# A decoder trunk on one core: a pinned prologue, the first scale on TensorE, and start-up units in sweeps

## The chip, the cores and the metric

The kernel runs on one core of a Trainium2 chip. The metric is the device time of one execution in microseconds, the median of several runs; smaller is better. The core's engines each run their own instructions in order and wait for each other by semaphores: TensorE (PE; its weight loads are shown as PEld), VectorE (DVE), ScalarE (ACT), GpSimd (POOL) and SyncE (SP), which issues all DMAs here.

## The reference

Two layers on x of 256 positions by 1024 channels. Each layer has three blocks: SwiGLU, a mixer (Mamba-2 in layer 0, block-sparse attention in layer 1), SwiGLU. Each block's input is normalized and modulated by a vector c:

```python
def modulate(x, g, c_act, w, b):
    m = c_act @ w + b
    shift, scale, gate = jnp.split(m, 3, axis=-1)
    h = rmsnorm(x, g) * (1.0 + scale[:, None, :]) + shift[:, None, :]
    return h, gate[:, None, :]

def swiglu(h, w_gate, w_up, w_down):
    return (jax.nn.silu(h @ w_gate) * (h @ w_up)) @ w_down
...
    c_act = jax.nn.silu(c)
    for i in range(DEPTH):
        h, g = modulate(x, norm_g[i, 0], c_act, mod_w[i, 0], mod_b[i, 0])
        x = x + 0.5 * g * swiglu(h, ffn_w_gate[i, 0], ffn_w_up[i, 0], ffn_w_down[i, 0])
...
    return rmsnorm(x, final_norm_g)
```

D_FF is 2816. All is float32.

## The kernel before

x lies transposed, channels on partitions: eight tiles of 128 channels by 256 positions. Every weight matrix is streamed once, in units of 16 blocks of 128 x 128 (1 MB), loaded by SP into three buffers `raw`. A product is kept near float32 accuracy by splitting both sides into a high part in a shorter format and the rest: `split` makes `hi` of a half unit (8 blocks, 128 x 1024) on ACT (line 309) and `lo = raw - hi` on DVE (line 316), and `make_x`, `pre_x` or, at the start, `first_x` make XH and XL of the activations. `prod` (lines 382 to 384) then issues three matmuls per block: hi by XH, hi by XL, lo by XH. Six `hi` and six `lo` buffers stand between the splits and TensorE.

The modulation vectors are made meanwhile: `modulation` multiplies a 128 x 1024 tile of the modulation matrix, `mraw`, by the broadcast c, `cb`, and sums along the row, in one instruction on DVE (line 340). `vectors` adds the bias (shift; line 325) or makes (acc + b1) * g (scale; line 327) into MV.

The first block cannot use vectors made ahead. So its first eight units (`ffn`, p == 0) go by input tile k: unit k holds the blocks of input tile k for eight output tiles m, gate and up. For each k a scale and a shift are made (tiles 8 + k and k), then `first_x` makes ut = x * scale * rb on DVE (line 1032), XH on ACT (line 1035) and XL on DVE (line 1036). `stream_order` sets the order of modulation tiles and units in ORDER; `pump` walks it, some half units ahead of TensorE; LOADS is the order of the DMAs.

Before that stands the prologue (the block "start"): the DMAs of V (vectors and biases), the identity and x; SiLU of c; eight transposes that broadcast c into two banks and two copies into `cb`; squares of x on ACT and DVE and their sums; eight one-column matmuls with `ones` (`rstd_sum`, line 393) for the mean square; the root on ACT (line 396) and four small DVE instructions; two transposes (`rstd_rows`) for the row vector `rb`. `early`, a manual schedule, is held from the start of this block to the first `pump`. From there on the scheduler sets the order of instructions on each engine by priority.

Of the kernel before, what the change touches and what calls it, by code (L numbers as in the profile page):

```python
# [146 lines left out]
def stream_order():  # L147
# [16 lines left out]
    for i in range(len(ALL_UNITS)):  # L164
        if i < NK:
            order += [("m", 0, 8 + i)] * (i < 2) + [("m", 0, i)] + [("m", 0, 9 + i)] * (1 <= i < NK - 1)
        order.append(("w", i))
        while n < len(items) and at[n] <= i + 1:
            order.append(("m",) + items[n])
            n += 1  # L170
# [7 lines left out]
LOADS += ORDER[3 * NK:3 * NK + 2] + [("c",)] + ORDER[3 * NK + 2:]  # L178
SLOT = {it: n % N_MOD for n, it in enumerate(it for it in LOADS if it[0] == "m")}
# [10 lines left out]

@with_exitstack
def hybrid_trunk(ctx, tc, w, mod, xt, vec, const, out, dbg=None):
# [3 lines left out]
    mm, act, dve, gps = nc.tensor, nc.scalar, nc.vector, nc.gpsimd  # L196
# [17 lines left out]
    b1 = pool.tile([128, 48], F32, name="b1")  # L214
    MV = pool.tile([128, 6, 3, NK], F32, name="MV")
# [10 lines left out]
    st = Core()  # L226
# [78 lines left out]
    def split(q):  # L305
# [45 lines left out]
    def pump(q):  # L351
# [3 lines left out]
        while st.s <= q:  # L355
# [29 lines left out]


    def rstd_sum(parts, n):
# [603 lines left out]
    with tc.tile_pool(name="start", bufs=1) as sp:  # L991
# [145 lines left out]
```

## Time and profile before

| what | us |
|---|---|
| median of 3 runs | 1114.82 |
| lowest and highest run | 1113.73, 1115.0 |
| the profiled execution | 1115.07 |
| its span | 1113.3 |
| PE busy | 1090.7 (98% of the span) |
| DVE busy | 897.4 (81%) |
| ACT busy | 602.4 (54%) |

The span goes from the first to the last instruction of the profiled execution; 1.77 us of its time lie around it. Ends of matmuls are modelled and overlap, so the spacing of their starts is what to read. In a timeline row the first number is the start, the second the duration; in brackets is the engine's idle time just before and what ended it. Instructions on DVE and ACT also overlap a little: the next can start before the last one's end. On the page, "us to landing" is from a DMA's issue to its data.

### The profile page before, as it was taken

To read this page: it belongs to the slowest core of one execution; us is meant where nothing else is said; L and a number is where in the kernel's file an instruction comes from. 1 tells how busy PE (TensorE), PEld (TensorE's weight loads), DVE (VectorE), ACT (ScalarE), POOL (GpSimd) and SP (SyncE) were. 2 spreads that over 40 slices of the span, in tenths; PEclk is the share of its full clock that TensorE was granted. 3 is DMA by queue.
4 is the path that set the end of the run, shared out by engine and by line. 5 is a ranking of instruction groups with operands and counts; after the bars stand their busy time and mean duration, and the time that the engine had idled before them with its cause. 6 is when DMAs were issued, how large, how long until landed. Compare 5 with 4: busy or idle time off the path is not lost.

```text
span 1113.3 us, 22076 instructions
## 1 busy us (share of the span) xinstructions
PE 1090.7 (98%) x9050; PEld 1067.7 (96%) x9050; DVE 897.4 (81%) x1445; ACT 602.4 (54%) x919; POOL 55.4 (5%) x61
## 2 busy tenths in 40 slices
PE   6999999999999998999999999999999999999997
PEld 6999999999899998999999999999988899999996
DVE  6998989899899999999976889886697779555542
ACT  4463445676776657444544644454475666444541
POOL 0000001000000001000001000001211210000010
PEclk9999999999999999999999999999999999999998
DMA  9989988853444663899966499986544336555531
GB/s 349 381 335 369 352 319 302 301 200 117 175 166 142 240 238 128 302 356 367 375 246 246 160 346 334 356 308 263 186 174 156 121 115 222 190 184 183 186 136 39
DMA packets 50358, 269.00 MB, mean 242 GB/s; under 512 B 5840, under 2 KB 6608, under 8 KB 28624
## 3 DMA queue, kind: packets, MB, share of 16 engines
q1 hardware_dynamic: 50256, 267.58, 65.4%
q8 instruction: 71, 1.16, 0.4%
q14 instruction: 31, 0.25, 0.1%
HBM read 266.51 MB, written 1.05 MB: 240 GB/s over the span
## 4 chain that ended last, share of the span: by engine, by line
PE 94%; DVE 4%; ACT 1%; issue 1%; DMA 0%; SPq 0%; DVEq 0%; ACTq 0%
PE bank L383 29%; PE bank L382 29%; PE bank L384 29%; PE bank L734 1%; DVE lo L316 1%; PE bank L957 1%; PE bank L959 1%; PE bank L958 1%; PE bank L874 1%; PE bank L393 1%; PE bank L915 1%; DVE x L458 0%; ACT hi L309 0%; DMA x<-in_xt_dram 0%; DVE X L439 0%
## 5 line engine op out<-in xcount | busy, mean ns | idle before, releaser
L316 DVE TENSOR_TENSOR lo<-raw,hi 128x1024 fp32r<-128x1024 f32 x361 | 437.7, 1221 | 136.9 <-ACT hi L309 136.6
L309 ACT ACTIVATE hi<-raw 128x1024 fp32r<-128x1024 f32 x361 | 376.8, 1057 | 310.8 <-PE bank L383 253.2
L383 PE MATMUL bank<-X,hi 128*128 128x256 f32 (+1 forms) x1928 | 542.7, 282 | 1.5 <-DVE X L439 1.4
L382 PE MATMUL bank<-X,hi 128*128 128x256 f32 (+1 forms) x1928 | 538.3, 282 | 4.0 <-ACT hi L309 2.5
L384 PE MATMUL bank<-X,lo 128*128 128x256 f32 (+1 forms) x1928 | 538.8, 281 | 0.2 <-DVE lo L316 0.2
L382 PEld LDWEIGHTS bank<-X,hi 128*128 128x128 f32 x1928 | 364.2, 190 | 8.6 <-issue 3.4
L383 PEld LDWEIGHTS bank<-X,hi 128*128 128x128 f32 x1928 | 363.7, 189 | 2.8 <-DVE X L439 1.8
L384 PEld LDWEIGHTS bank<-X,lo 128*128 128x128 f32 x1928 | 363.4, 189 | 0.4 <-DVE lo L316 0.4
L384 PE MATMUL bank<-H,lo 128*128 128x256 f32 x704 | 196.9, 280 | 0.0
L382 PE MATMUL bank<-H,hi 128*128 128x256 f32 x704 | 196.3, 279 | 0.0
L383 PE MATMUL bank<-H,hi 128*128 128x256 f32 x704 | 196.2, 279 | 0.0
L340 DVE SCALAR_TENSOR_TENSOR junk<-mraw,cb 128x1024 bf16<-128x1024 f32 x144 | 175.4, 1218 | 0.9 <-DMA mraw<-in_mod_dram 0.2
L383 PEld LDWEIGHTS bank<-H,hi 128*128 128x128 f32 x704 | 132.3, 188 | 0.0
L384 PEld LDWEIGHTS bank<-H,lo 128*128 128x128 f32 x704 | 132.1, 188 | 0.0
L382 PEld LDWEIGHTS bank<-H,hi 128*128 128x128 f32 x704 | 131.6, 187 | 0.0
L416 POOL TENSOR_TENSOR ssq<-ssq,sq 128x256 f32<-128x256 f32 x36 | 34.4, 955 | 966.3 <-ACT sq L414 965.8
L522 ACT ACTIVATE sg<-bank 128x512 f32<-128x512 f32 x41 | 24.0, 585 | 38.9 <-PE bank L384 38.9
L634 DVE SCALAR_TENSOR_TENSOR cv<-bank,V,cv 128x255 f32<-128x255 f32 (+2 forms) x96 | 44.3, 474 | 0.5
L458 DVE SCALAR_TENSOR_TENSOR x<-bank,MV,x 128x256 f32<-128x256 f32 x40 | 19.1, 480 | 29.2 <-PE bank L384 29.1
L414 ACT ACTIVATE sq<-x 128x256 f32<-128x256 f32 x36 | 14.9, 414 | 50.6 <-DVE x L458 45.9
L382 PE MATMUL bank<-GH,hi 128*128 128x256 f32 x128 | 36.2, 284 | 1.1 <-DVE cv L634 0.9
L384 PE MATMUL bank<-GH,lo 128*128 128x256 f32 x128 | 36.0, 282 | 0.0
(179 smaller groups left out, 924.1 us busy)
## 6 DMA issues: line engine op xcount, KB each, us to landing
raw<-in_w_dram SPq DMA_DIRECT2D x169, 1024.0 KB, 5.1
mraw<-in_mod_dram SPq DMA_DIRECT2D x144, 512.0 KB, 6.5
raw<-in_w_dram SPq DMA_DIRECT2D x23, 512.0 KB, 8.1
x<-in_xt_dram SPq DMA_DIRECT2D x2, 512.0 KB, 4.6
out_dram<-x SPq DMA_DIRECT2D x3, 256.0 KB, 2.3
out_dram<-x SPq DMA_DIRECT2D x2, 128.0 KB, 1.9
V<-in_vec_dram SPq DMA_DIRECT2D x1, 196.5 KB, 8.3
mask<-in_const_dram SPq DMA_DIRECT2D x1, 192.0 KB, 8.1
```

Of the source, the lines that this page charges most:

```text
L309: act.activation(h, r, AF.Copy)
L316: ins = dve.tensor_sub(l[:, c:wd], r[:, c:wd], h[:, c:wd].bitcast(F32)).ins
L340: ins = dve.scalar_tensor_tensor(junk, mraw[SLOT["m", j, c]], 1.0, cb, op0=OP.mult, op1=OP.mult, accum_out=acc[:, j, c:c + 1]).ins
L382: mm.matmul(ps, h, xh, start=start, stop=False, skip_group_check=True)
L383: mm.matmul(ps, h, xl, start=False, stop=False, skip_group_check=True)
L384: mm.matmul(ps, l, xh, start=False, stop=stop, skip_group_check=True)
L393: mm.matmul(ps[:, t:t + 1], s[:, 128 * t:128 * t + 128], ones[:, c:c + 1], start=e == 0 and t == 0, stop=e == len(parts) - 1, skip_group_c ...
L414: act.activation(s, src, AF.Square)
L416: gps.tensor_add(total, total, s)
L458: dve.scalar_tensor_tensor(x[:, d, :], ps, g, x[:, d, :], op0=OP.mult, op1=OP.add)
L522: act.activation(s, ps[:, :, :L], AF.Silu)
L634: dve.scalar_tensor_tensor(o[:, c, s:], ps[:, c, :L - s], V[:, wc + 3 - s:wc + 4 - s], o[:, c, s:], op0=OP.mult, op1=OP.add)
```

## The change

- The identity comes no longer by DMA: POOL fills it with ones and selects the diagonal (`affine_select`).
- The first scale (tile 8) is made by eight one-column matmuls on TensorE from its `mraw` tile and c; the host stores that tile transposed. It no longer needs DVE.
- Each half of the squares is summed to one 256-column tile by one more DVE addition, so the mean square takes four one-column matmuls and not eight. The load of the root's table moves ahead on ACT.
- 23 transposes into an unused bank (`warm`) are put between TensorE's steps of the prologue.
- The scale and shift of the eight input tiles are finished on ACT, (acc * g + b1 * g) and (acc + b), and not on DVE.
- In ORDER the scale product of unit k + 1 stands right behind the split of the first half of unit k, the shift product behind its second half.
- A wrapper, `Pinned`, keeps all instructions of PE, DVE and ACT in program order from the start until the second half of the last of the eight units. (All instructions that go through the wrapper show its line, L202, where the kernel's own line stood.)
- `sweeps` replaces `prod` in the eight units: for each half unit eight matmuls hi by XH, eight hi by XL, eight lo by XH.

```diff
@@ stream_order
         if i < NK:
-            order += [("m", 0, 8 + i)] * (i < 2) + [("m", 0, i)] + [("m", 0, 9 + i)] * (1 <= i < NK - 1)
-        order.append(("w", i))
+            order += [("m", 0, 8)] * (i == 0) + [("m", 0, i)]
+        order += [("w", i), ("m", 0, 9 + i)] if i < NK - 1 else [("w", i)]
@@
+class Pinned:
...
+        def call(*args, **kw):
+            ins = f(*args, **kw)
+            if self.st.pin:
+                self.tc.keep_in_program_order(ins)
+            return ins
+        return call
@@ hybrid_trunk
-    mm, act, dve, gps = nc.tensor, nc.scalar, nc.vector, nc.gpsimd
+    st = Core()
+    st.pin = False
+    mm, act, dve = (Pinned(tc, e, st) for e in (nc.tensor, nc.scalar, nc.vector))
+    gps = nc.gpsimd
@@ split
-        act.activation(h, r, AF.Copy)
-        if st.pending:
-            st.pending()
-            st.pending = None
+        if q:
+            act.activation(h, r, AF.Copy)
+            if st.pending:
+                st.pending()
+                st.pending = None
...
         ins = dve.tensor_sub(l[:, c:wd], r[:, c:wd], h[:, c:wd].bitcast(F32)).ins
...
+        if q == 0:
+            st.pending()
+            st.pending = None
@@ vectors
-        if kind == 0:
+        if k1 == k0 + 1:
+            if kind:
+                act.activation(o, a if src is None else src, AF.Identity, scale=V[:, V_NG + k0:V_NG + k1], bias=b1g[:, k0:k1])
+            else:
+                act.activation(o, a, AF.Identity, bias=V[:, c + k0:c + k1])
+        elif kind == 0:
             dve.tensor_add(o, a, V[:, c + k0:c + k1])
-        elif kind == 1 and k1 == k0 + 1:
-            dve.tensor_scalar(o, a, b1[:, 8 * j + k0:8 * j + k1], V[:, V_NG + 32 * j + k0:V_NG + 32 * j + k1],
-                              op0=OP.add, op1=OP.mult)
@@ pump
                 split(st.s)
+                if st.s % 2 == 0 and st.s < 2 * NK - 2:
+                    modulation(*ORDER[st.p + 1][1:])
...
-                    st.p += 1
+                    st.p += 2 if st.s < 2 * NK - 1 else 1
@@
+    def sweeps(i, b, outs, xh, xl, start, stop):
+
+        for n, ps in enumerate(outs):
+            mm.matmul(ps, weights(i, b + n)[0], xh, start=start and n % 2 == 0, stop=False, skip_group_check=True)
+        for n, ps in enumerate(outs):
+            mm.matmul(ps, weights(i, b + n)[0], xl, start=False, stop=False, skip_group_check=True)
+        for n, ps in enumerate(outs):
+            mm.matmul(ps, weights(i, b + n)[1], xh, start=False, stop=stop, skip_group_check=True)
@@ ffn
-                    for m in range(8):
-                        for s in range(2):
-                            prod(bs[m // 2][:, m % 2, L * s:L * s + L], k, 2 * m + s, XH[:, k, :L], XL[:, k, :L],
-                                 k == 0 and s == 0, k == NK - 1)
-                        if k == NK - 1 and m % 2:
-                            evac(m - 1, bs[m // 2])
+                    for q in range(2):
+                        sweeps(k, SUB * q, [bs[m // 2][:, m % 2, L * s:L * s + L] for m in range(4 * q, 4 * q + 4) for s in range(2)],
+                               XH[:, k, :L], XL[:, k, :L], k == 0, k == NK - 1)
+                        if k == NK - 1:
+                            st.pin = False
+                            evac(4 * q, bs[2 * q])
+                            evac(4 * q + 2, bs[2 * q + 1])
@@ the block "start"
-        early = ExitStack()
-        early.enter_context(tc.manual_schedule())
+        st.pin = True
         nc.sync.dma_start(V[:, :V_MB + 32], vec[:, :V_MB + 32])
-        nc.sync.dma_start(ident, const[:, 0:128])
...
+        gps.memset(ident, 1.0)
+        gps.affine_select(ident, ident, [[-1, 128]], OP.is_equal, 0.0, base=0, channel_multiplier=1)
...
         act.activation(ca, V[:, V_C:V_C + 8], AF.Silu)
+        preload(AF.Sqrt, False)
...
+        dve.tensor_mul(b1g, b1[:, :8], V[:, V_NG:V_NG + 8])
...
+        def warm(n):
+
+            for _ in range(n):
+                mm.transpose(idle[:, :128], ident, ident)
+
+        def sums(s, start):
+            for t in range(2):
+                mm.matmul(ps[:, t:t + 1], s[:, 128 * t:128 * t + 128], ones[:, 0:1], start=start and t == 0,
+                          stop=not start, skip_group_check=True)
+
+        def scale0(k0, k1):
+
+            for k in range(k0, k1):
+                mm.matmul(pm[:, 0:1], mraw[SLOT["m", 0, 8]][:, 128 * k:128 * k + 128], ca[:, k:k + 1], start=k == 0,
+                          stop=k == NK - 1)
...
+        warm(6)
+        act.activation(cb[:, :512], pc[0], AF.Copy)
         for h in range(2):
...
             dve.tensor_add(sq0[:, c:c + 2], sq0[:, c:c + 2], sq0[:, c + 2:c + 4])
+            dve.tensor_add(sq0[:, c], sq0[:, c], sq0[:, c + 1])
             if h == 0:
-                for q in range(2):
-                    act.activation(cb[:, 512 * q:512 * q + 512], pc[q], AF.Copy)
-        preload(AF.Sqrt, False)
-        modulation(*ORDER[0][1:])
-        r = rstd_sum([sq0[:, c, :] for c in (0, 1, 4, 5)], D)
+                act.activation(cb[:, 512:], pc[1], AF.Copy)
+                sums(sq0[:, 0], True)
+                warm(3)
+                scale0(0, 4)
+            else:
+                sums(sq0[:, 4], False)
+                scale0(4, 8)
+        root(ps)
+        st.m += 1
+        vectors(0, 1, 0, 1, pm[:, 0:1])
         modulation(*ORDER[1][1:])
-        rstd_rows(r, True)
+        r = rstd(ps)
+        for t in range(2):
+            mm.transpose(pr[:, 128 * t:128 * t + 128], r[:, t:t + 1].to_broadcast([128, 128]), ident)
+        warm(14)
+        act.activation(hi[0], raw[0][:, :128 * SUB], AF.Copy)
```

Left out of the diff: the two names that `rstd_sum` is cut into (`root` is its ACT instruction, `rstd` its four of DVE), the host's transposition of one tile, and in `first_x` that ut of tile 0 reads the bank and not `rb`.

ACT in the start-up units, before: `hi` of half units 3 to 6 with X of input tiles 2 and 3.

```order
L309 ACTIVATE hi_67<-raw_62 128x1024
L309 ACTIVATE hi_68<-raw_63 128x1024
L1035 ACTIVATE X<-ut_101,MV 128x256
L309 ACTIVATE hi_69<-raw_63 128x1024
L309 ACTIVATE hi_64<-raw_61 128x1024
L1035 ACTIVATE X<-ut_99,MV 128x256
```

ACT in the start-up units, after: half units 2 to 5, with X of input tile 2.

```order
L202 ACTIVATE hi_66<-raw_62 128x1024
L202 ACTIVATE MV<-acc,b1g,V 128x1
L202 ACTIVATE hi_67<-raw_62 128x1024
L202 ACTIVATE MV<-acc,V 128x1
L202 ACTIVATE X<-ut_102,MV 128x256
L202 ACTIVATE hi_68<-raw_63 128x1024
L202 ACTIVATE MV<-acc,b1g,V 128x1
L202 ACTIVATE hi_69<-raw_63 128x1024
```

Two `hi` stood between one X and the next, the later of them for the unit of the X behind it; now the `hi` of a unit's first half stands behind X, that of its second half behind an MV, and X behind another MV.

DVE in one round before: modulation tiles of unit 2 (scale, then shift), ut, the two `lo` of the unit with the low part of X between them.

```order
L340 SCALAR_TENSOR_TENSOR junk,acc<-mraw_80,cb 128x1024
L327 TENSOR_SCALAR MV<-acc,b_92,V 128x1
L340 SCALAR_TENSOR_TENSOR junk,acc<-mraw_76,cb 128x1024
L1032 SCALAR_TENSOR_TENSOR ut_101<-x,MV,rb 128x256
L325 TENSOR_TENSOR MV<-acc,V 128x1
L316 TENSOR_TENSOR lo_74<-raw_63,hi_68 128x1024
L1036 SCALAR_TENSOR_TENSOR X<-ut_101,MV,X 128x256
L316 TENSOR_TENSOR lo_75<-raw_63,hi_69 128x1024
```

DVE in one round after: `lo` of the first half of unit 1, scale product of unit 2, ut, `lo` of the second half, shift product, low part of X, `lo` of unit 2.

```order
L202 TENSOR_TENSOR lo_72<-raw_62,hi_66 128x1024
L202 SCALAR_TENSOR_TENSOR junk,acc<-mraw_80,cb 128x1024
L202 SCALAR_TENSOR_TENSOR ut_102<-x,MV,rb 128x256
L202 TENSOR_TENSOR lo_73<-raw_62,hi_67 128x1024
L202 SCALAR_TENSOR_TENSOR junk,acc<-mraw_76,cb 128x1024
L202 SCALAR_TENSOR_TENSOR X<-ut_102,MV,X 128x256
L202 TENSOR_TENSOR lo_74<-raw_63,hi_68 128x1024
```

The two products stood together and ut behind the second; now a `lo` and a step that reads ACT's result follow each product.

PE from the start to the first weight matmuls, before.

```order
L1011 MATMUL bank<-ident,ca 128x128 x8
L393 MATMUL bank<-ones,sq_110 128x1 x8
L406 MATMUL bank<-ident,sm 128x128 x2
L382 MATMUL bank<-X,hi_64 128x256
L383 MATMUL bank<-X,hi_64 128x256
L382 MATMUL bank<-X,hi_64 128x256
```

PE from the start into unit 0, after (`ident` alone as input: `warm`; `ca,mraw`: the first scale).

```order
L202 MATMUL bank<-ident,ca 128x128 x8
L202 MATMUL bank<-ident 128x128 x6
L202 MATMUL bank<-ones,sq_111 128x1 x2
L202 MATMUL bank<-ident 128x128 x3
L202 MATMUL bank<-ca,mraw_76 128x1 x4
L202 MATMUL bank<-ones,sq_111 128x1 x2
L202 MATMUL bank<-ca,mraw_76 128x1 x4
L202 MATMUL bank<-ident,sm 128x128 x2
L202 MATMUL bank<-ident 128x128 x14
L202 MATMUL bank<-X,hi_64 128x256 x16
L202 MATMUL bank<-X,lo_70 128x256 x8
```

Four one-column matmuls for the sums are gone, eight for the scale and 23 transposes have come, and the weight matmuls stand in runs of 16 with `hi` and 8 with `lo`.

## Rows read from the trace of the kernel before

**Rows 1.** The page, part 1: busy us, share of the span, instructions of each engine.
```profile
PE 1090.7 (98%) x9050; PEld 1067.7 (96%) x9050; DVE 897.4 (81%) x1445; ACT 602.4 (54%) x919; POOL 55.4 (5%) x61
```

**Rows 2.** Waits of PE, whole run (line and releaser: us in all, times, longest).
```profile
PE bank L383 <- DVE X L439: 1.4, 2, 0.8
...
PE bank L384 <- DVE lo L316: 0.2, 1, 0.2
```

**Rows 3.** Windows: stretch, then busy us (count) by engine, PEclk, DMA share, GB/s.
```profile
15.50:21.43 5.93, 5.92 (x27) 5.92 (x28) 5.89 (x10) 2.44 (x4) 0.00 (x0) 1.00 1.02 409
30.00:36.00 6.00, 6.00 (x53) 6.00 (x52) 5.96 (x11) 2.78 (x4) 0.00 (x0) 1.00 1.03 410
```

**Rows 4.** Timeline of the prologue: start us, duration us, engine, line [idle before].
```profile
1.16 0.42 SPq L998 DMA_DIRECT2D ident<-in_const_dram  x1
5.83 0.69 DVE L1015 TENSOR_TENSOR sq<-x 128x512 f32<-128x512 f32 x1 [3.08 <-DMA x<-in_xt_dram]
7.47 3.54 PE L393 MATMUL bank<-ones,sq 128*128 128x1 f32 x16 [1.50 <-DVE sq L1016]
8.92 1.23 DVE L340 SCALAR_TENSOR_TENSOR junk<-mraw,cb 128x1024 bf16<-128x1024 f32 x1 [0.20 <-DMA mraw<-in_mod_dram]
11.12 0.26 ACT L396 ACTIVATE sm<-bank,eps 128x2 f32<-128x2 f32 x1 [1.65 <-PE bank L393]
12.29 0.69 PE L406 MATMUL bank<-ident,sm 128*128 128x128 f32 x2 [1.27 <-DVE sm L400]
14.41 1.99 ACT L309 ACTIVATE hi<-raw 128x1024 fp32r<-128x1024 f32 x2
15.51 0.58 PE L382 MATMUL bank<-X,hi 128*128 128x256 f32 x1 [2.53 <-ACT hi L309]
```

**Rows 5.** The chain that ended last, PE's pieces (start us, us).
```profile
16.30 0.21 PE bank L382
24.16 0.60 PE bank L382 x5
58.28 0.59 PE bank L382 x5
```

**Rows 6.** Timeline of DVE in one round of the start-up units.
```profile
42.49 1.22 DVE L340 SCALAR_TENSOR_TENSOR junk<-mraw,cb 128x1024 bf16<-128x1024 f32 x1
43.63 0.08 DVE L340 DVE_READ_ACCUMULATOR junk<-mraw,cb 128x1 f32 x1
43.63 0.48 DVE L1032 SCALAR_TENSOR_TENSOR ut<-x,MV,rb 128x256 f32<-128x256 f32 x1
44.02 0.15 DVE L325 TENSOR_TENSOR MV<-acc,V 128x1 f32<-128x1 f32 x1
44.09 1.22 DVE L316 TENSOR_TENSOR lo<-raw,hi 128x1024 fp32r<-128x1024 f32 x1
45.23 0.48 DVE L1036 SCALAR_TENSOR_TENSOR X<-ut,MV,X 128x256 fp32r<-128x256 f32 x1
48.30 1.22 DVE L340 SCALAR_TENSOR_TENSOR junk<-mraw,cb 128x1024 bf16<-128x1024 f32 x1
```

**Rows 7.** Timeline of ACT in the same round.
```profile
44.21 0.51 ACT L1035 ACTIVATE X<-ut,MV 128x256 fp32r<-128x256 f32 x1 [1.89 <-DVE MV L325]
44.63 1.99 ACT L309 ACTIVATE hi<-raw 128x1024 fp32r<-128x1024 f32 x2
```

**Rows 8.** POOL's line 416 (min/median/max ns), DMA queues to 30 us, DMA issues.
```profile
L416 POOL TENSOR_TENSOR ssq<-ssq,sq x36: 732/808/1427, 160.1 to 1097.0; 128x256 f32<-128x256 f32 x36
L416 POOLq MODIFY_POOL_CONFIG  x2: 11/11/11, 0.9 to 0.9; - x2
q8 instruction: 1, 0.02, 0.2%
V<-in_vec_dram SPq DMA_DIRECT2D x1, 196.5 KB, 8.3
ident<-in_const_dram SPq DMA_DIRECT2D x1, 64.0 KB, 2.7
```

More of the change, by code (lines that the diff above doesn't have):

```diff
@@ L178 @@
 LOADS += ORDER[3 * NK:3 * NK + 2] + [("c",)] + ORDER[3 * NK + 2:]
+assert sorted(LOADS[:3 * NK]) == sorted(ORDER[:3 * NK])
 SLOT = {it: n % N_MOD for n, it in enumerate(it for it in LOADS if it[0] == "m")}
@@ L188, with __init__, __getattr__ @@
     pass
+class Pinned:
+    def __init__(self, tc, engine, st):
+        self.tc, self.engine, self.st = tc, engine, st
+    def __getattr__(self, name):
+        f = getattr(self.engine, name)
+        def call(*args, **kw):
[4 more added lines that the diff above has]
+        return call
 @with_exitstack
@@ L214, in hybrid_trunk @@
     b1 = pool.tile([128, 48], F32, name="b1")
+    b1g = pool.tile([128, NK], F32, name="b1g")
     MV = pool.tile([128, 6, 3, NK], F32, name="MV")
@@ L225, in hybrid_trunk @@
     psum = psp.tile([128, 8, 512], F32, name="bank")
-    st = Core()
     st.bank = 0
@@ L318, in split, with vectors @@
             st.sub = ins
-    def vectors(j, kind, k0, k1):
+        if q == 0:
+            st.pending()
+            st.pending = None
+    def vectors(j, kind, k0, k1, src=None):
         o, a = MV[:, j, kind, k0:k1], acc[:, j, 8 * kind + k0:8 * kind + k1]
         c = V_MB + 32 * j + 8 * kind
-        if kind == 0:
+        if k1 == k0 + 1:
[4 more added lines that the diff above has]
+        elif kind == 0:
             dve.tensor_add(o, a, V[:, c + k0:c + k1])
-        elif kind == 1 and k1 == k0 + 1:
-            dve.tensor_scalar(o, a, b1[:, 8 * j + k0:8 * j + k1], V[:, V_NG + 32 * j + k0:V_NG + 32 * j + k1],
-                              op0=OP.add, op1=OP.mult)
         elif kind == 1:
@@ L394, in rstd_sum, with root, rstd @@
                           stop=e == len(parts) - 1, skip_group_check=True)
+        root(ps)
+        return rstd(ps)
+    def root(ps):
+        act.activation(sm[:, 0:2], ps[:, 0:2], AF.Sqrt, bias=eps)
+    def rstd(ps):
         q, r, t = (sm[:, 2 * i:2 * i + 2] for i in range(3))
-        act.activation(q, ps[:, 0:2], AF.Sqrt, bias=eps)
         dve.reciprocal(r, q)
@@ L1007, in hybrid_trunk @@
         act.activation(ca, V[:, V_C:V_C + 8], AF.Silu)
+        preload(AF.Sqrt, False)
         dve.tensor_scalar(b1[:, :8], V[:, V_MB + 8:V_MB + 16], 1.0, None, op0=OP.add)
+        dve.tensor_mul(b1g, b1[:, :8], V[:, V_NG:V_NG + 8])
         pc = [bank(), bank()]
+        idle, ps, pm, pr = bank(), bank(), bank(), bank()
+        def warm(n):
[9 more added lines that the diff above has]
+                          stop=k == NK - 1)
         for k in range(NK):
             mm.transpose(pc[k // 4][:, 128 * (k % 4):128 * (k % 4) + 128], ca[:, k:k + 1].to_broadcast([128, 128]), ident)
+        warm(6)
+        act.activation(cb[:, :512], pc[0], AF.Copy)
         for h in range(2):
@@ L1016, in hybrid_trunk @@
             dve.tensor_add(sq0[:, c:c + 2], sq0[:, c:c + 2], sq0[:, c + 2:c + 4])
+            dve.tensor_add(sq0[:, c], sq0[:, c], sq0[:, c + 1])
             if h == 0:
-                for q in range(2):
-                    act.activation(cb[:, 512 * q:512 * q + 512], pc[q], AF.Copy)
-        preload(AF.Sqrt, False)
-        modulation(*ORDER[0][1:])
-        r = rstd_sum([sq0[:, c, :] for c in (0, 1, 4, 5)], D)
-        modulation(*ORDER[1][1:])
-        rstd_rows(r, True)
+                act.activation(cb[:, 512:], pc[1], AF.Copy)
[5 more added lines that the diff above has]
+                scale0(4, 8)
+        root(ps)
+        st.m += 1
+        vectors(0, 1, 0, 1, pm[:, 0:1])
+        modulation(*ORDER[1][1:])
+        r = rstd(ps)
[3 more added lines that the diff above has]
+        act.activation(hi[0], raw[0][:, :128 * SUB], AF.Copy)
     st.p = 2
@@ L1031, in first_x @@
             st.u[k] = utmp()
-            dve.scalar_tensor_tensor(st.u[k], x[:, k, :], MV[:, j, 1, k:k + 1], rb, op0=OP.mult, op1=OP.mult)
+            dve.scalar_tensor_tensor(st.u[k], x[:, k, :], MV[:, j, 1, k:k + 1], rb if k else pr[:, :L], op0=OP.mult, op1=OP.mult)
         else:
@@ L1040, in hybrid_trunk @@
     first_x(0, 0)
+    act.activation(rb, pr[:, :L], AF.Copy)
     st.on_mod = first_x
     pump(0)
-    early.close()
     ffn(0, 0)
@@ L1091, in host_arrays @@
     mod = np.ascontiguousarray(inp["mod_w"].reshape(6, D, 3 * D).transpose(0, 2, 1))
+    first = inp["mod_w"].reshape(6, D, 3 * D)[0, :, D:D + 128]
+    mod[0, D:D + 128] = first.reshape(NK, 128, 128).transpose(1, 0, 2).reshape(128, D)
     vec = np.zeros((128, V_COLS), np.float32)
```

## The prediction

> **What bounds the kernel now.** I read the page first. TensorE (PE) is busy 98% of the span [rows 1], so a change pays only where it makes TensorE start earlier, run faster or wait less. Next I read who TensorE waits for: after its first weight matmul at 15.51 us [rows 4] its first wait is 0.2 us for a `lo` tile, at 70 us [rows 2]. Between lie the eight start-up units that the change rewrites, 384 matmuls. They end about 63.9 us: a burst of five matmuls marks each unit's beginning, the one at 24.16 us belongs to unit 1 and the one at 58.28 us to unit 7, so a unit takes 34.12 / 6 = 5.69 us, 0.1187 us a matmul, and unit 7 ends about 5.6 us after its burst [rows 5].
>
> The windows say what is close behind: VectorE (DVE) is busy 5.96 of 6.00 us there [rows 3], and its own round, from one shift product (L340) to the next, is 48.30 - 42.49 = 5.81 us [rows 6]. It has no wait in that round. TensorE hides this because it begins at half speed: its first matmuls stand 0.21 us apart [rows 5], the 1.2 GHz level (256 columns), though the granted clock reads 1.00 there too [rows 3]; from 21.4 us on they stand 0.12 us apart. By then VectorE is ahead. ScalarE (ACT) has time: it sat idle 1.89 us before X [rows 7]. So in this stretch two engines are full, and any wait put into VectorE's round lengthens it at once.
>
> **The change, part by part.** *The round of the first eight units* decides, so it comes first. Off VectorE go the two small results of a unit, about 0.3 us with their handoff: the addition alone is 0.15 us [rows 6]. They become ScalarE instructions. The order fences show what that does in a fixed order: on ScalarE the `hi` of a unit's second half stands behind MV of the scale, which needs VectorE's scale product; X stands behind MV of the shift; the next `hi` behind X. On VectorE each `lo` needs the `hi` just made, and the next product stands behind that `lo`. Before, `hi` ran ahead and VectorE did `lo` while ScalarE made X. Now it is one chain through both engines. With m the start of a scale product:
> - product to its accumulator 1.14 + 0.08 = 1.22 [rows 6]; handoff 0.04 (the addition ends 44.17, X begins 44.21 [rows 6, 7]);
> - MV, priced by the nearest small ScalarE row, 0.26 [rows 4]; the `hi` behind it may begin 0.09 before its end, as `hi` does behind X [rows 7], so 0.17;
> - `hi` 1.05 (two take 1.99 [rows 7]), handoff 0.04, `lo` to the next instruction 1.14 [rows 6]. Half a round: 3.66;
> - shift product 1.22 + 0.04, MV with its handoff 0.30, X until `hi` may begin 0.42, `hi` 1.05, handoff 0.04, `lo` 1.14. Second half: 4.21.
>
> Together 7.87 us a unit against 5.69 us that TensorE needs. VectorE's own work fits between (0.40 for ut and 0.48 for the low part of X [rows 6]); it then waits some 2.3 us a unit. The estimate lies between VectorE's work alone, about 5.6 (5.81 less the results), and this chain with 0.1 more at each of eight handoffs, 8.7. I take the chain, since it is what the order forces and every link but MV has its row here.
>
> *The prologue.* The identity's DMA goes, so x is issued 0.42 us and a gap earlier [rows 4]: at 5.4 instead of 5.83. VectorE squares and adds twice 0.69 and then 0.40 (a 256-column instruction [rows 6]) per half: halves ready at 7.4 and 9.3. One-column matmuls cost 3.54 / 8 = 0.44 us each [rows 4]; there were eight, now four sums and eight that make the first scale. The first four of these need the first modulation tile, 8.92 less 0.45, and stand behind three fillers: 8.9 to 10.7; then the second sums to 11.6, the other four to 13.3. The root and four VectorE steps run beside these. Two transposes 0.69 [rows 4] to 14.0, ut to 14.5. On ScalarE the two MV fill 13.35 to 13.9, `hi` ends 14.9, X at 15.3. VectorE ends `lo` at 16.1 and the low part at 16.55. TensorE could begin at 15.3 instead of 15.51, and if the fillers keep it awake, at 0.12 us a matmul: worth 28 x 0.095 = 2.7 us where TensorE is the bound. It no longer is, so I count the earlier start and the clock at nothing; 3 us of fillers are hidden by the same slack. Were the product's chain gone they would show.
>
> *The sweeps* do not alter the count of 384; they let 16 of 24 matmuls of a half run before `lo`. The wait is for `hi` and X, which sweeps don't shorten. The scheduler also moves one split of unit 8 ahead of unit 7's low part of X: 1.14 us beside MV and X, 0.4 us net. The 40-column b1, now between two rounds, waits for a late DMA; 0 to 2.6 us, taken as nothing, since the queue is emptier when units take longer. Loading bounds no round: the DMA share is full now at one unit per 5.69 us, so a unit needs that or less.
>
> *The sum.* First scale product of unit 1 at 16.55; six rounds, 47.2, bring unit 7's to 63.8. There X and `hi` are ready 6.73 us later (3.66 + 1.22 + 0.04 + 0.30 + 0.42 + 1.05 + 0.04), and 48 matmuls take 5.70 at the fast level; the last two `lo` are ready in time for their sweeps. Unit 7 ends at 63.8 + 12.4 = 76.2, 12.3 us later than now. Behind it the order is the same but for a few rows and TensorE is full, so nothing is won back. The profiled execution took 1115.07 us, 0.25 above the median of the runs: 1127.4 there, **1127.1 us** against the median of 1114.82. Doubt on the handoffs (0.2 a round, six rounds) and the prologue (a faster TensorE there ends it up to 2.3 us earlier) makes 1124 to 1130.
>
> **The rule that speaks against the identity.** Here the trace shows the library call of GpSimd (POOL) at 0.9 us, 11 ns long, and its first user only at 160.1 us, 0.73 to 1.43 us each; on the instruction queue there is one packet in the first 30 us [rows 8]. A start-up would have been hidden. The Trainium skill, GPSIMD Engine Reference, section 2.1 (Instruction dispatch), says that the first call to a freshly loaded kernel pays about 6 us; no run here shows it. By that the identity would come at about 7.5 us (an estimate from that page), and the sum would be some 3.5 us more.
>
> **The rivals.**
> - *The identity is late.* It now heads TensorE's queue, and ScalarE's copy of c behind it stands ahead of the squares. Until 4.2 us it costs nothing (eight transposes before x at 5.4); later, each us counts. The nearest rows for a fetch from memory are 2.7 us (ident's own landing) and 8.3 us (V, in a full queue) [rows 8]; from 0.95 us on, with 0.8 for the select, it comes at 4.4 to 10: up to 5.8 us more, the middle 3. Then about 1130.5. For it: it is on the path with nothing to hide it. Against: the single packet.
> - *The clock falls in the gaps.* TensorE idles 2.2 of 7.9 us. It was at 1.2 GHz after a mostly idle prologue; a wait of 0.8 us later on [rows 2] left it fast. If unit 7 runs slow, 48 x 0.095 = 4.6 us more: 1131.7.
> - *The handoffs hide and the kernel is faster.* If ScalarE's steps cost VectorE no time, a round is 5.6, TensorE's 5.69 bounds, and it starts at 15.3 and fast: unit 7 ends at 15.3 + 8 x 5.69 = 60.8, 3.1 us sooner, 1111.7. It decides at a round of 5.8: 16.55 + 6 x 5.8 + 12.4 = 63.8 is now's end. For it: VectorE's work does shrink. Against: the order, in which four ScalarE results a unit are waited for with nothing between.
> - *The order does less than it says*: rounds of about 5.8 and the prologue's gain spent in it, no difference.
>
> **How the numbers follow.** Chain as summed 0.53; late identity on top 0.25; slow clock on top 0.10; faster 0.07; no difference 0.05. About 0.2% (2.2 us) is what a measurement of this kernel tells from no change. Slower 0.88, same 0.05, faster 0.07. The range takes the first three: 1123 to 1134, from the chain with a quick prologue and short handoffs to a late identity or slow clock.
>
> **What would show it.** In the profile after: rounds of 7.9 us between scale products, with VectorE idle some 2.3 us of each, released by ScalarE's `hi`, X and MV; TensorE idle some 2 us per unit between 20 and 75 us, waiting for `hi`; the identity at about 2 us, or late. Rounds under 6 us, or unit 7 ending before 65 us, make the prediction wrong.

## The result and the profile after

The changed kernel takes 1133.52 us (median of four runs, 1133.3 to 1136.13), beside 1114.91 us for the kernel before on the same chip (1113.73 to 1116.13): a ratio of 1.0171, 95% interval 1.0159 to 1.0183. The sign and the mechanism at the start were as forecast, but the loss is 18.6 us where the sum gave 12.3. The profiled execution took 1133.67 us, its span 1131.9. The page's first part answers to [rows 1]; TensorE's waits in the start-up (15 to 80 us) to [rows 2]:

```profile
PE 1103.7 (98%) x9081; PEld 1078.8 (95%) x9081; DVE 896.1 (79%) x1430; ACT 609.0 (54%) x935; POOL 55.5 (5%) x63
```
```profile
PE bank L202 <- ACT hi L202: 11.6, 13, 1.2
```

TensorE now waits 13 times for a `hi`, 11.6 us in all, where the kernel before had one wait for a `hi`, ahead of its first weight matmul, and 0.2 us for a `lo`. Yet it is also busy 13.0 us longer (1103.7 against 1090.7) with the same matmuls on weights; the last fourteen fillers (the transposes of `warm`) account for 3.0 of that (a row below), the other nine for 2.4. So more than waits has come in.

One round of VectorE, scale product to scale product, answers to [rows 6] (start us, duration us, idle before and its releaser in brackets):

```profile
39.67 1.22 DVE L202 SCALAR_TENSOR_TENSOR junk<-mraw,cb 128x1024 bf16<-128x1024 f32 x1
40.81 0.08 DVE L202 DVE_READ_ACCUMULATOR junk<-mraw,cb 128x1 f32 x1
41.35 0.48 DVE L202 SCALAR_TENSOR_TENSOR ut<-x,MV,rb 128x256 f32<-128x256 f32 x1 [0.46 <-ACT MV L202]
42.30 1.23 DVE L202 TENSOR_TENSOR lo<-raw,hi 128x1024 fp32r<-128x1024 f32 x1 [0.47 <-ACT hi L202]
43.44 1.22 DVE L202 SCALAR_TENSOR_TENSOR junk<-mraw,cb 128x1024 bf16<-128x1024 f32 x1
44.58 0.08 DVE L202 DVE_READ_ACCUMULATOR junk<-mraw,cb 128x1 f32 x1
45.57 0.49 DVE L202 SCALAR_TENSOR_TENSOR X<-ut,MV,X 128x256 fp32r<-128x256 f32 x1 [0.91 <-ACT X L202]
46.52 1.22 DVE L202 TENSOR_TENSOR lo<-raw,hi 128x1024 fp32r<-128x1024 f32 x1 [0.46 <-ACT hi L202]
47.66 1.22 DVE L202 SCALAR_TENSOR_TENSOR junk<-mraw,cb 128x1024 bf16<-128x1024 f32 x1
```

A round is 47.66 - 39.67 = 7.99 us, 5.81 before. Four waits, 0.46 + 0.47 + 0.91 + 0.46 = 2.30 us, each for ScalarE, are the difference. ScalarE in the same round answers to [rows 7]; it waits 2.44 us for each product, so neither engine is full, and the two take turns:

```profile
40.93 0.39 ACT L202 ACTIVATE MV<-acc,b1g,V 128x1 f32<-128x1 f32 x1 [2.44 <-DVE junk L202]
41.22 1.04 ACT L202 ACTIVATE hi<-raw 128x1024 fp32r<-128x1024 f32 x1
44.70 0.29 ACT L202 ACTIVATE MV<-acc,V 128x1 f32<-128x1 f32 x1 [2.44 <-DVE junk L202]
45.03 0.51 ACT L202 ACTIVATE X<-ut,MV 128x256 fp32r<-128x256 f32 x1
45.44 1.04 ACT L202 ACTIVATE hi<-raw 128x1024 fp32r<-128x1024 f32 x1
```

TensorE's timeline (answering to [rows 4, 5]): fillers to the first unit, a half unit in the middle, and the first matmuls of unit 8.

```profile
12.93 3.02 PE L202 MATMUL bank<-ident 128*128 128x128 f32 x14
15.70 2.13 PE L202 MATMUL bank<-X,hi 128*128 128x256 f32 x16
...
42.32 2.17 PE L202 MATMUL bank<-X,hi 128*128 128x256 f32 x16 [0.66 <-ACT hi L202]
...
76.36 0.40 PE L202 MATMUL bank<-X,hi 128*128 128x256 f32 x2
```

Units are counted from 0, so the eight units are 0 to 7. Unit 8 begins at 76.36 us; in the kernel before it begins with matmul 385 of the weights at 63.74. So 12.6 us are lost up to there. From there to the start of the last matmul on weights it takes 1121.71 - 76.36 = 1045.35 us, and 1103.34 - 63.74 = 1039.60 before: 5.75 us more, with the same matmuls and no new wait. The rest, 0.2 us, lies behind that matmul.

Where these 5.75 us go is seen by tiles. This is the first down projection, 528 matmuls on H without a gap (line, tiles, count, duration ns min/median/max, first and last start us). Of the kernel before, its third part, and of the changed kernel:

```profile
L384 PE MATMUL bank<-H,lo x176: 278/280/280, 143.6 to 205.4; 128*128 128x256 f32 x176
```
```profile
L202 PE MATMUL bank<-H,lo x176: 281/281/285, 155.7 to 218.7; 128*128 128x256 f32 x176
```

Between the first and the last start lie 175 x 3 = 525 matmuls: 61.8 / 525 = 117.7 ns each before, 63.0 / 525 = 120.0 ns now. There are 2112 matmuls on H, so this makes some 4.8 us. Added up over all distances between starts, H takes 4.6 us more and GH, GL, OH and OL, some 570 matmuls, 1.4 more; all else together takes 0.3 less. The mean distance of starts on X is 118.2 ns in both. H, GH, GL, OH and OL lie behind the pool "main", which grew by the 32 bytes of `b1g`; X lies ahead of `b1g` and did not move. That made the theory for the experiments: what counts is the place of the moving operand (the activations, H or X, that stream past the loaded weights).

### The profile page after: what moved, and what is told of

Read it like the earlier page. It is cut to its first block, busy times and chain, and to the rows that moved or that the text cites. A ratio compares the mean times of both kernels' runs of the same rounds, so it can differ in the third digit from the quotient of the medians.

```text
span 1131.9 us, 22185 instructions
## 1 busy us (share of the span) xinstructions
PE 1103.7 (98%) x9081; PEld 1078.8 (95%) x9081; DVE 896.1 (79%) x1430; ACT 609.0 (54%) x935; POOL 55.5 (5%) x63
## 4 chain that ended last, share of the span: by engine, by line
PE 90%; DVE 4%; ACT 3%; issue 2%; DMA 1%; DVEq 0%; SPq 0%; ACTq 0%
PE bank L202 90%; ACT hi L202 2%; DVE junk L202 1%; DVE lo L202 1%; DVE x L202 1%; DMA raw<-in_w_dram 0%; DVE X L202 0%; DVE ut L202 0%; ACT wt L202 0%; ACT MV L202 0%; DMA x<-in_xt_dram 0%; DVE cv L202 0%; ACT th L202 0%; DVE sq L202 0%; DVE wt L202 0%
## 5 line engine op out<-in xcount | busy, mean ns | idle before, releaser
L202 PE MATMUL bank<-X,hi 128*128 128x256 f32 (+1 forms) x3856 | 681.0, 282 | 14.6 <-ACT hi L202 11.6
L202 PEld LDWEIGHTS bank<-X,hi 128*128 128x128 f32 x3856 | 583.2, 189 | 22.8 <-ACT hi L202 14.3
L202 ACT ACTIVATE hi<-raw 128x1024 fp32r<-128x1024 f32 x361 | 379.5, 1058 | 342.7 <-PE bank L202 279.7
L202 DVE TENSOR_TENSOR lo<-raw,hi 128x1024 fp32r<-128x1024 f32 x361 | 439.2, 1223 | 149.8 <-ACT hi L202 149.1
L202 PE MATMUL bank<-X,lo 128*128 128x256 f32 (+1 forms) x1928 | 521.7, 281 | 0.0
L202 PEld LDWEIGHTS bank<-X,lo 128*128 128x128 f32 x1928 | 354.7, 188 | 0.0
L202 PE MATMUL bank<-H,hi 128*128 128x256 f32 x1408 | 253.6, 281 | 0.0
L202 PEld LDWEIGHTS bank<-H,hi 128*128 128x128 f32 x1408 | 218.1, 189 | 0.0
L202 PE MATMUL bank<-H,lo 128*128 128x256 f32 x704 | 199.2, 283 | 0.0
L202 DVE SCALAR_TENSOR_TENSOR junk<-mraw,cb 128x1024 bf16<-128x1024 f32 x143 | 174.1, 1218 | 1.6 <-DMA mraw<-in_mod_dram 0.9
L202 PEld LDWEIGHTS bank<-H,lo 128*128 128x128 f32 x704 | 131.6, 187 | 0.0
L202 DVE SCALAR_TENSOR_TENSOR cv<-bank,V,cv 128x255 f32<-128x255 f32 (+2 forms) x96 | 44.4, 474 | 0.4
L202 DVE SCALAR_TENSOR_TENSOR x<-bank,MV,x 128x256 f32<-128x256 f32 x40 | 19.1, 481 | 30.0 <-PE bank L202 30.0
L202 PE MATMUL bank<-GH,hi 128*128 128x256 f32 x128 | 36.6, 287 | 1.2 <-DVE cv L202 0.9
L202 ACT ACTIVATE sq<-x 128x256 f32<-128x256 f32 (+1 forms) x38 | 16.1, 425 | 40.0 <-DVE x L202 37.8
L202 PE MATMUL bank<-GH,lo 128*128 128x256 f32 x128 | 36.4, 284 | 0.0
L202 PE MATMUL bank<-GL,hi 128*128 128x256 f32 x128 | 36.1, 282 | 0.0
L202 ACT ACTIVATE H<-hh 128x512 fp32r<-128x512 f32 (+1 forms) x47 | 27.8, 593 | 14.6 <-DVE hh L202 14.6
L202 ACT ACTIVATE sg<-bank 128x512 f32<-128x512 f32 x41 | 23.8, 583 | 19.9 <-PE bank L202 19.9
L202 DVE SCALAR_TENSOR_TENSOR X<-x,MV,X 128x256 fp32r<-128x256 f32 x40 | 28.0, 702 | 5.9 <-ACT X L202 5.8
L202 DVE TENSOR_TENSOR H<-hh,H 128x512 fp32r<-128x512 f32 (+1 forms) x47 | 30.4, 650 | 1.0 <-ACT H L202 1.0
```

The costliest lines, as they stand in the source:

```text
L202: ins = f(*args, **kw)
```

## The experiments

Matmul 385 marks the end of the eight units ("unit 7 ends"). The ratios are to the kernel before, run beside each experiment: 1115.6 to 1115.9 us.

**The place of H and of all else behind "main", in the kernel before** (before_shift).

```diff
     SC = pool.tile([128, 4], F32, name="SC")
+    spare = pool.tile([128, 8], F32, name="spare")
```

> The kernel before with one more tile of 32 bytes per partition behind the last tile of the pool 'main', used by nothing: H, GH, GL, OH and OL begin 32 bytes further on, all else stays where it was. Theory (the address at which these operands begin sets how fast TensorE reads them; the change moved it by the 32 bytes of b1g): about 6 us slower, near 1121 us, matmuls on H 119.9 to 120.1 ns apart instead of 117.6 to 117.9, those on X unchanged at 118.1, unit 7 still ending near 63.9 us. Rival (the slower matmuls come from what the change does at the start, or from the small tiles MV, acc and the rest that also moved): no difference, 1114.9 us, H at 117.8 ns.

Measured: 1120.37 us, ratio 1.0048 (1.0033 to 1.0063). The same row as above:

```profile
L385 PE MATMUL bank<-H,lo x176: 278/281/285, 142.5 to 205.5; 128*128 128x256 f32 x176
```

63.0 / 525 = 120.0 ns, X at 118.1. From unit 8 to the last matmul on weights it takes 1045.56 us, 6.0 more than in the kernel before. Unit 7 ends at 62.6 and not at 63.7, mostly as 18 of the first matmuls stand at the 1.2 GHz level (0.21 us apart) here and 28 in the profile before. Thirty-two unused bytes cost 5.4 us by the ratio. The theory holds; the rival falls.

**The place of H back to a multiple of 64 bytes, in the changed kernel** (after_back): the same line added there.

> The changed kernel with the same unused tile of 32 bytes behind the last one of 'main', so that H and its like begin at a multiple of 64 bytes again; b1g, MV, acc and the rest stay where the change put them. Theory (address of H): 6.1 us less than the changed kernel, near 1127.4 us, H back at 117.6 to 117.9 ns, the start-up unchanged (rounds 7.99 us, unit 7 ends at 76.4). Rival (the moved small tiles or the start): 1133.5 us, H still near 120 ns.

Measured: 1133.66 us, 1.0166 (1.0151 to 1.0181), no gain.

```profile
L202 PE MATMUL bank<-H,lo x176: 284/284/284, 155.5 to 218.5; 128*128 128x256 f32 x176
```

Again 63.0 us. The expectation was wrong: a multiple of 64 is not what makes the place good. Either the place goes by a finer rule or the changed kernel has another cause; the next run tells these apart.

**All tiles at their old places, in the changed kernel** (after_addr).

```diff
-    b1g = pool.tile([128, NK], F32, name="b1g")
...
     acc = pool.tile([128, 6, 24], F32, name="acc")
+    b1g = acc[:, 5, 16:24]
```

> The changed kernel with b1g not in a tile of its own but in eight columns of acc that are used only much later (those of the last block's gate): every tile has the address that it has in the kernel before; instructions and their order are those of the changed kernel. Two shifts (32 and 64 bytes) both left matmuls on H 120 ns apart, so 64-byte alignment as such is not it. Theory (the place of H, by some finer rule, sets it): H back at 117.6 to 117.9 ns, near 1127.5 us. Rival (in the changed kernel the slow H has another cause, though a shift can do it too): H stays near 120 ns, 1133.5 us.

Measured: 1127.08 us, 1.0112 (1.0096 to 1.0129).

```profile
L202 PE MATMUL bank<-H,lo x176: 278/280/280, 155.4 to 217.2; 128*128 128x256 f32 x176
```

61.8 us, as before; unit 8 to the last matmul on weights 1039.26 us, as before. With the instructions and the order unchanged, 6.4 us are gone. What is left, 11.5 us over the 1115.59 us beside it, is the start-up: unit 7 ends at 75.94 us.

**Which places are good** (before_shift128): a tile of 32 float32 as `spare`.

> The kernel before with an unused tile of 128 bytes per partition behind the last one of 'main': H and its like begin 128 bytes further on. If the place within 128 bytes sets it: H at 117.8 ns, 1114.9 us. If only this one place is good, or the place within 256 bytes sets it: H near 120 ns, 1121 us.

Measured: 1104.34 us, 0.9909 (0.9894 to 0.9925), faster than anything so far.

```profile
L385 PE MATMUL bank<-H,lo x176: 276/276/276, 142.4 to 201.9; 128*128 128x256 f32 x176
```

59.5 / 525 = 113.3 ns: neither case that was expected. From unit 8 to the last matmul on weights it takes 1030.16 us, 9.4 less than in the kernel before; of the rest of the 11.3 us, 1.2 lie in the start-up, which shows fewer slow matmuls again (19). By bytes ahead of H: 0 gives 117.7 ns, 32 and 64 give 120.0, 128 gives 113.3.

**X moved too** (before_shiftX): the 128 bytes stand ahead of X, so all tiles from X on move with it.

> The kernel before with the unused tile of 128 bytes ahead of X instead of behind the last tile: X moves by 128 bytes as well, H and its like lie as in before_shift128. Each of the eight XH and XL lies 16 or 8 bytes further on within 128 bytes than the one before it, so X already sees many places. If the place within 256 bytes sets the matmuls on X too: they leave their 118.1 ns, and each ns on some 5,200 of them is 5.2 us; H at 113.1 to 113.8 ns. If only H and its like have such a rule, or X's places average out: X at 118.1 ns, near 1104.3 us.

Measured: 1112.55 us, 0.9973 (0.9964 to 0.9983). H keeps its 113 ns; X gives back most of what H won. Lines, PE (busy us, mean ns): of before_shift128, then of before_shiftX.

```profile
L385 PE MATMUL bank<-X,lo 128*128 128x256 f32 (+1 forms) x1928 | 538.3, 281 | 0.2 <-DVE lo L317 0.2
```
```profile
L385 PE MATMUL bank<-X,lo 128*128 128x256 f32 (+1 forms) x1928 | 545.1, 284 | 0.1
```

By starts, X goes from 118.2 (`hi` and `lo`) to 119.0 and 120.7 ns. So the rule is not one of H alone.

**The small results back on VectorE** (after_mvdve): after_back with

```diff
-        if k1 == k0 + 1:
-            if kind:
-                act.activation(o, a if src is None else src, AF.Identity, scale=V[:, V_NG + k0:V_NG + k1], bias=b1g[:, k0:k1])
-            else:
-                act.activation(o, a, AF.Identity, bias=V[:, c + k0:c + k1])
+        if k1 == k0 + 1 and src is None and kind:
+            dve.tensor_scalar(o, a, b1[:, 8 * j + k0:8 * j + k1], V[:, V_NG + 32 * j + k0:V_NG + 32 * j + k1],
+                              op0=OP.add, op1=OP.mult)
...
         elif kind == 0:
```

> after_back with the scale and shift vectors of units 1 to 7 back on VectorE (unit 0's scale stays on ScalarE), all in the same fixed order. Theory (the round is one chain through VectorE and ScalarE): the handoffs to the two small results go, and hi of a second half no longer stands behind one, so the lo of that half finds it ready; left are the waits for X and for the hi behind it. Round: 1.22 + 0.15 + 0.40 + 1.14 for the scale half, 1.22 + 0.15 + 1.51 + 1.14 for the shift half = 6.93 us; unit 7 ends near 69, about 7.5 us sooner, near 1120 us. Rival (the fixed order or the sweeps as such make the round): rounds of 8 us stay, 1127.4 us.

Measured: 1134.95 us, 1.0177 (1.0161 to 1.0192). VectorE:

```profile
42.84 1.22 DVE L202 SCALAR_TENSOR_TENSOR junk<-mraw,cb 128x1024 bf16<-128x1024 f32 x1
...
47.95 0.49 DVE L202 SCALAR_TENSOR_TENSOR X<-ut,MV,X 128x256 fp32r<-128x256 f32 x1 [0.58 <-ACT X L202]
48.89 1.22 DVE L202 TENSOR_TENSOR lo<-raw,hi 128x1024 fp32r<-128x1024 f32 x1 [0.46 <-ACT hi L202]
50.04 1.22 DVE L202 SCALAR_TENSOR_TENSOR junk<-mraw,cb 128x1024 bf16<-128x1024 f32 x1
...
59.20 0.20 DVE L202 TENSOR_SCALAR b<-V 128x40 f32<-128x40 f32 x1 [5.97 <-DMA V<-in_vec_dram]
```

The round did fall, to 50.04 - 42.84 = 7.20 us (6.93 expected), with two waits left in place of four. But the time did not: the 40-column `b1`, fixed in the order, now stands 5.97 us ahead of its late load of V, and TensorE waits 8.4 us. Here the place of H was the one of after_back, so its 6 us are in this time too.

**The same instructions in another fixed order** (after_order): after_back with

```diff
@@ split
         if q:
             act.activation(h, r, AF.Copy)
-            if st.pending:
-                st.pending()
-                st.pending = None
+        if i >= NK and st.pending:
+            st.pending()
+            st.pending = None
+        if q % 2 and q < 2 * NK - 2:
+            modulation(0, 8 + i + 1)
+        elif 0 < q < 2 * NK and q % 2 == 0:
+            modulation(0, i)
...
-        if q == 0:
+        if q < 2 * NK and st.pending:
             st.pending()
             st.pending = None
```

`ut` is made by `st.pending` too, behind the lo, and `pump` no longer calls `modulation` behind a split.

> after_back with another fixed order in the eight units, the same instructions: lo of a half stands between the product of the next vector and what needs that vector, so VectorE has 1.14 us of work while ScalarE makes MV and X; hi stands ahead of MV on ScalarE. Theory (the chain was the loss): no wait is left in VectorE's round, 2 x 1.22 + 2 x 1.14 + 0.40 + 0.48 = 5.60 us, TensorE's 5.69 us bounds, and since it starts near 15.7 us and at the full clock unit 7 ends near 61.2 us instead of 63.9: 1112.4 us, faster than both kernels. Rival (the loads, 2 MB a unit, cannot come faster than in the kernel before, 5.7 us a unit or more): rounds near 6 us, unit 7 ends at 63.4, 1114.6 us.

Measured: 1127.88 us, 1.0114 (1.0097 to 1.0131). VectorE in one round, and where it ends:

```profile
38.16 1.21 DVE L202 SCALAR_TENSOR_TENSOR junk<-mraw,cb 128x1024 bf16<-128x1024 f32 x1
...
39.30 1.21 DVE L202 TENSOR_TENSOR lo<-raw,hi 128x1024 fp32r<-128x1024 f32 x1
40.44 0.47 DVE L202 SCALAR_TENSOR_TENSOR ut<-x,MV,rb 128x256 f32<-128x256 f32 x1
40.83 1.21 DVE L202 SCALAR_TENSOR_TENSOR junk<-mraw,cb 128x1024 bf16<-128x1024 f32 x1
...
53.96 1.22 DVE L202 TENSOR_TENSOR lo<-raw,hi 128x1024 fp32r<-128x1024 f32 x1 [7.37 <-ACT hi L202]
```

The waits are gone but for one of 0.25 us, and a round (two products) is 5.36 us, from 32.80 to 38.16: each small result is ready when VectorE comes to its reader. Then VectorE stands 7.37 us: the second half of unit 8, which is no longer held in order, was put ahead of the splits of units 6 and 7, and its `hi` waits for its load on ScalarE. TensorE then waits 5.11 us, and the 16 matmuls behind that wait take 3.48 us and not some 2.1, at the 1.2 GHz level (granted clock 0.50 from 57 to 59 us):

```profile
52.87 1.06 ACT L202 ACTIVATE hi<-raw 128x1024 fp32r<-128x1024 f32 x1 [6.43 <-DMA raw<-in_w_dram]
57.36 3.48 PE L202 MATMUL bank<-X,hi 128*128 128x256 f32 x16 [5.11 <-ACT X L202]
```

So the forecast of the round held and that of the time did not. The place of H is that of after_back here too.

**Order, places and these two waits mended** (best): after_order with `b1g` in `acc` and no spare tile, and

```diff
                         if k == NK - 1:
-                            st.pin = False
+                            if q == 1:
+                                st.pin = False
+                                late_b1()
```

where `late_b1` is the 40-column b1.

> after_order, with three edits: b1g in acc, so that all addresses are those of the kernel before; the fixed order kept until the last of the eight units is done, so that no later split can be put ahead; the 40-column b1, which waits for a late load, behind that point. In after_order TensorE ran without a wait until VectorE stood 7.37 us before a lo of unit 8 that the scheduler had put ahead of units 6 and 7. Theory: no wait in the eight units, TensorE's 5.70 us a unit bounds, start 14.9 to 16.8 (the first loads land up to 2 us apart), unit 7 ends at 60.5 to 62.4 us, H at 117.8 ns: 1111.7 to 1113.6 us, faster than both. Rival (the loads cannot keep this pace): waits of hi for raw from unit 4 on, unit 7 near 64, 1115 us.

Measured: 1113.98 us, 0.9986 (0.9977 to 0.9994): faster than the kernel before by a little, and by 19.5 us than the changed one. TensorE at its first weights and at the start of unit 8:

```profile
15.04 2.56 PE L202 MATMUL bank<-X,hi 128*128 128x256 f32 x16
...
60.95 0.40 PE L202 MATMUL bank<-X,hi 128*128 128x256 f32 x2
```

Unit 7 ends at 60.95, as expected: 2.8 us sooner than in the profile before, but only 1.6 sooner than in its three shifted versions (62.5 to 62.6), and 1.6 us is also what the medians differ by. Up to the last matmul on weights 0.6 us is given back; 0.4 of it is one wait for a `lo` at 67 us.

**Without the fillers** (best_nowarm): best with `pass` in place of the loop in `warm`.

> best without the 23 transposes into an unused bank. Theory (they keep the clock up): the first weight matmul comes some 1.2 us sooner, but stands at the 1.2 GHz level for about 28 matmuls, which cost 0.095 us more each, so unit 7 ends 1.5 us later than in best: 1113.5 to 1115 us. Rival (the small matmuls that stay keep the clock up as well): 1.2 us sooner than best.

Measured: 1114.21 us, 0.9996 (0.9987 to 1.0006).

```profile
14.76 3.52 PE L202 MATMUL bank<-X,hi 128*128 128x256 f32 x16 [1.44 <-ACT X L202]
```

The first weights come 0.28 us sooner and the first 16 matmuls take 3.52 us and not 2.56: they stand at the 1.2 GHz level (0.21 us apart) for longer, 14 matmuls and not 4. Unit 7 ends at 61.65, 0.7 us later (1.5 expected). The two medians can't be told apart; in this pair of traces the fillers are worth 0.7 us, less than the first weights move from one profile to another.

**The order left to the scheduler behind the prologue** (after_free): after_addr with `st.pin = False` ahead of the first `pump`.

> after_addr with the fixed order kept only through the prologue; from the first split on the scheduler orders the same instructions (sweeps and small results on ScalarE stay). By its order a split and two products of later units come ahead of the last steps of unit 0 on VectorE, so TensorE starts later, near 17.5 us; from then on a product or a lo stands between a small result and its reader in most places. Theory (the loss at the start is the fixed order alone, not the sweeps or the moved small results): rounds at TensorE's 5.70 us, unit 7 ends near 63, about 1114.5 us. Rival (the small results on ScalarE cost their handoffs in any order): rounds of 6.5 us or more, 1120 us or more.

Measured: 1118.44 us, 1.0027 (1.0016 to 1.0038). VectorE at the start, and the `lo` of two rounds near the end:

```profile
14.21 1.20 DVE L202 TENSOR_TENSOR lo<-raw,hi 128x1024 fp32r<-128x1024 f32 x1
15.34 0.15 DVE L202 SCALAR_TENSOR_TENSOR sm<-sm 128x2 f32<-128x2 f32 x1
...
49.86 1.23 DVE L202 TENSOR_TENSOR lo<-raw,hi 128x1024 fp32r<-128x1024 f32 x1 [0.91 <-ACT hi L202]
...
56.34 1.23 DVE L202 TENSOR_TENSOR lo<-raw,hi 128x1024 fp32r<-128x1024 f32 x1 [0.91 <-ACT hi L202]
```

Large steps stand between the small ones of the prologue, and the first weight matmul comes at 21.30 us. From there unit 7 ends at 67.98: 46.7 us, 5.83 a unit (6.99 the first, which begins at the lower clock), with no further wait of TensorE up to 100 us. So TensorE lost nothing to the sweeps or the small results there. VectorE did: its last two rounds took 6.48 us each (the later one 56.34 - 49.86), longer than TensorE's units, with 0.91 us of waiting for a `hi` that stands behind an MV on ScalarE. That is the rival's round; it stayed hidden because TensorE began some 6 us later than in best and VectorE was ahead. That the small results need not cost VectorE anything is shown by after_order, not by this run. The start was expected 3.8 us too early.

**Both gains together** (best_shift128), and the place 256 bytes on (best_shift256).

> best with the unused tile of 128 bytes, so that H begins 128 bytes further on, where matmuls on H stood 113.1 to 113.8 ns apart in before_shift128 (1104.34 against 1115.59 us). Theory (the two gains are in different stretches and add): 1113.98 - 11.25 = 1102.7 us, faster than every kernel so far. Rival (they do not add, VectorE or the loads bind where TensorE gets faster): 1104 us or more.

> best with an unused tile of 256 bytes: H begins 256 bytes further on than in the kernel before. If the place within 256 bytes sets the matmuls on H: 117.6 to 117.9 ns, 1114 us as best. If the period is longer: another spacing, and a time that moves by some 2.6 us for each ns.

best_shift128: 1104.51 us, 0.9898 (0.9881 to 0.9914), no faster than before_shift128. In its profile the start is late (first weights at 16.19 us) and TensorE drops to the 1.2 GHz level once (windows as in [rows 3]; TensorE was busy 0.57 of the 2 us from 434, and granted clock 0.50 is the lower level):

```profile
434.00:436.00 2.00, 0.57 (x5) 0.36 (x3) 1.92 (x6) 1.79 (x4) 0.00 (x0) 1.00 0.85 360
438.00:440.00 2.00, 2.00 (x11) 2.00 (x11) 2.00 (x6) 0.85 (x2) 0.00 (x0) 0.50 0.00 0
```

Whether the 1.6 us that best gains over the kernel before went this way in the other runs can't be told from one profile; that the two gains add is not shown. best_shift256: 1114.26 us, 0.9986 (0.9976 to 0.9995), the time of best:

```profile
L202 PE MATMUL bank<-H,lo x176: 278/280/280, 141.4 to 203.3; 128*128 128x256 f32 x176
```

61.9 us, as with no shift at all: a place 256 bytes on behaves the same.

## Why the prediction was right and where it was wrong

- *The round as one chain.* "Together 7.87 us a unit": 7.99 in the trace, as forecast in kind and size. The links were right but for MV, taken as 0.26 from the nearest small row: 0.39 with two pointer operands and 0.29 with one, 0.16 more together. The wait of VectorE, "some 2.3 us a unit", was 2.30. after_order shows that the order made it: the same instructions took 5.36 us a round.
- *The start.* "First scale product of unit 1 at 16.55": 15.69. x was there at 4.61 and not 5.4, the first scale ran from 8.18 and not 8.9, and TensorE was done with it at 12.6 and not 13.3. ("Halves ready at 7.4 and 9.3" does not follow from the prediction's own terms, which give 7.2 and 9.0.) Over the eight kernels with this prologue and its fillers the first matmul of the scale comes from 7.75 to 9.22 us, mostly when its tile lands, and the first weights from 14.57 to 16.81, so this term can't be had to better than a microsecond.
- *The end of unit 7.* "76.2": 76.36. That it is so close is luck: two errors cancel (0.86 sooner at the start, 0.83 later over six rounds, which took 48.05 us). (The "0.1187 us a matmul" is 34.12 / 288 = 0.1185; it changes nothing.)
- *The clock.* The first 16 matmuls stand at the fast level (2.13 us), and the waits of 0.6 to 1.2 us in the rounds did not end it (granted clock 1.00 from 20 to 77 us): this rival fell. The fast start was in part luck: in the seven other profiles with this prologue 4 to 11 of the first matmuls stand at 0.21 us. A longer wait did end it, 5.11 us in after_order.
- *The late identity.* This rival, with 0.25, fell at the first row of GpSimd:

```profile
1.17 0.29 POOL L1046 TENSOR_SCALAR_AFFINE_SELECT ident<-ident 128x128 f32<-128x128 f32 x1
```

  The identity is ready at 1.5 us, and TensorE's first transposes, at 2.90, wait for `ca`. The 6 us that the Trainium skill, GPSIMD Engine Reference, section 2.1, gives for the first call to a freshly loaded kernel did not appear for this instruction: the library call (MODIFY_POOL_CONFIG) stands 0.06 us ahead of it, at 1.11 us.
- *The 40-column b1.* Taken as nothing "since the queue is emptier when units take longer": it starts at 59.42 without a wait. The cover was named rightly: in after_mvdve, with quicker units, it is gone and the wait is 5.97 us.
- *The step that failed.* "Behind it the order is the same but for a few rows and TensorE is full, so nothing is won back." That priced the 8088 matmuls behind the start-up at their old spacing. They have the same order but not the same operands' places: `b1g`, one line of the diff, moved H and its like by 32 bytes, and 5.75 us were lost. No rival held this. That the range (1123 to 1134) took in 1133.5 is luck: it reached up for a late identity and a slow clock, and neither came; the doubt that was given for the chain, 1124 to 1130, does not hold the result. With the places put back, after_addr takes 1127.08 us, so the 12.3 us for the parts that were summed stand.

## What to carry to other kernels

An order that is fixed must keep a long instruction between a small result on another engine and its reader; the same instructions took 7.99 or 5.36 us a round by their order, and what is not held in order can jump ahead into the gap. A new tile, however small, moves every tile behind it: compare the spacing of matmuls by tile before and after a change, far from the place of the change, before explaining a loss by its instructions. Where TensorE is full, trying a few places for its largest moving operand may be worth more than a better prologue: here 128 unused bytes took 9.4 us from the matmuls behind the start-up.

## What the hardware showed that was not expected

- The start-to-start distance of matmuls with 256 columns of float32r depends on where the moving operand begins: 113.3, 117.7 or 120.0 ns on H, for places 128, 0 (and 256) or 32 and 64 bytes on from the one in the kernel before. The Trainium skill, TensorE: Matmul & The Clock Gate, Part 1, states the columns over 2.4 GHz plus some 2.5 ns for back-to-back matmuls; for 256 columns that is an estimate of 109.2 ns. Here every matmul has a weight load of its own, and no place that was tried reached it.
- Only shifts by multiples of 32 bytes were tried, with the weights, `hi` and `lo`, where they were; the other tiles of H's pools, and in before_shiftX all tiles from X on, moved along. Why a place is good, and whether it is the distance to the weights or the place itself, stays open; it was not tried to move the weights or to give each part of X a place of its own.
- How long the first matmuls stay at the 1.2 GHz level differs between profiles: 28, 18, 19 and 16 of them, 0.21 us apart, in the kernel before and its three shifted versions, whose prologue is the same. One profile does not price a slow start.
- A wait in which TensorE was busy 0.57 of 2 us was followed by the 1.2 GHz level in best_shift128 (438 to 440 us) and not in before_shift128, which has the same wait at the same place.
